# First norm of a 512-token model: shifts by GpSimd products summed on ScalarE, five early weight chunks accumulated feature by feature, the context loaded later

## The chip, the cores and the metric

The kernel runs on one core of a Trainium2 chip. TensorE multiplies matrices, VectorE and ScalarE work elementwise, GpSimd does so too, SyncE issues the loads. The metric is the device time of one execution in microseconds; the median of three runs counts.

## The reference

Two transformer blocks over 512 tokens of 1024 features. What matters here is the beginning: the first norm, modulated by a shift and a scale that come from the conditioning vector `c`, and the first feed-forward part, whose weights it meets.

```python
cond = jax.nn.silu(c)
mod = (cond @ ada_w[i] + ada_b[i]).reshape(B, N_SUB, N_MOD, D_MODEL)
shift, scale, gate = mod[:, :, 0], mod[:, :, 1], mod[:, :, 2]
h = modulate(rms_norm(x, norm_g[i, 0]), shift[:, 0], scale[:, 0])      # rms_norm(x) * (1 + scale) + shift
x = x + 0.5 * gate[:, 0, None, :] * swiglu(h, ffn_w_in[i, 0], ffn_w_out[i, 0])
...
a, b = jnp.split(h @ w_in, 2, axis=-1)                                 # swiglu
return (jax.nn.silu(a) * b) @ w_out
```

The second block also reads a context of 256 tokens (`ctx_2`), which it normalizes and modulates in the same way.

## The kernel before

The 1024 features lie on 8 tiles of 128 partitions (here: features 0 to 7), the 512 tokens along the free dimension. `x` is normalized by a row `nR` of reciprocal roots, which GpSimd makes by a power (`nr`) and TensorE spreads over the partitions. Each feature of the normed `h` is kept as two parts, `hh` rounded and `hl` the rest, and each weight chunk of 128x1024 likewise as `whi` (ScalarE) and `wlo` (VectorE); `mm3` makes three matmuls of 512 columns of each pair, and `proj` runs them over the 8 features into one output tile, so 24 matmuls for a chunk.

`first_norm` goes through the features k. It loads two slices of `ada_w` of 128x1024: `ads` for the scale, `adh` for the shift. The scale is a product with `cond` (the SiLU of `c`, on all partitions) that VectorE also sums up (`ada_col`). The shift of features 0 to 3 is made by TensorE instead: `adh` comes in another layout (`shift`) and 8 matmuls of one column multiply it with `ck`. That of features 4 to 7 goes by `ada_col`. Then VectorE adds the biases, makes the gain `gs`, and `norm_apply` gives `hn` (VectorE), `hh` (ScalarE) and `hl` (VectorE):

```python
nc.vector.scalar_tensor_tensor(u, src, gs[:, k:k + 1], R, ALU.mult, ALU.mult)
nc.scalar.activation(hi, u, AF.Identity, bias=sh[:, k:k + 1])
nc.vector.scalar_tensor_tensor(lo, u, sh[:, k:k + 1], hi.bitcast(F32), ALU.add, ALU.subtract)
```

Behind features 1 to 5 one chunk each of the first feed-forward weights is loaded and split (`PRELOAD_AT`); `ffn` takes these five as the chunks of its first three pairs j and loads the others itself. The pools hold 4 raw chunks and 5 split ones, and 6 output tiles. All loads are issued by SyncE in one order (`load`); `ctx_norm` issues the context's load with no such tie, and does the context's squares late in the second layer. The order in which the engines' instructions stand is set by a scheduler from the written order and their dependencies. In the rows, L204 to L206 are the three matmuls of `mm3`, L458 the matmuls of the shift, L249 and L250 `ada_col`, L462 the gain, L199 and L200 the split.

Of the kernel before, what the change touches and what calls it, by code (L numbers as in the profile page):

```python
# [9 lines left out]
F32 = mybir.dt.float32  # L10
F32R = mybir.dt.float32r
U8 = mybir.dt.uint8
AF = mybir.ActivationFunctionType
# [22 lines left out]
PRELOAD_AT = (1, 2, 3, 4, 5)  # L36
SHIFTS_ON_PE = 4
# [63 lines left out]
def layout(inp):  # L101
# [14 lines left out]
    out["shift"] = tiles(a["ada_w"][0, :, :D])  # L116
# [49 lines left out]
class Builder:  # L166
# [165 lines left out]
    def out_rows(self, load, xs, gate, slots=()):  # L332
        """tail(seg, acc): x += gate * (W^T xs) and its sums of squares, the last rows by segments."""
        ws, nt = [], min(TAIL, self.wbufs) + len(slots)

        def tail(seg, acc):
            if not ws:
                for m in range(KT - nt):
                    w = load(m)
                    ps = self.psum()  # L340
                    self.proj(ps, w, xs)
                    self.residual(m, ps, gate(), FULL, acc)
                own = list(slots) + [None] * (nt - len(slots))
                ws.extend(load(m, slots=own[m - KT + nt]) for m in range(KT - nt, KT))
            for m, w in zip(range(KT - nt, KT), ws):
                ps = self.psum()
                self.proj(ps[:, :seg[1]], w, xs, seg)
                self.residual(m, ps, gate(), seg, acc)

        return tail  # L350

# [1 line left out]
    def ffn(self, layer, s, h, gate, fill, mid=None):  # L353
        nc, d = self.nc, self.d
        tail = None
        for pi, (j0, n) in enumerate(PARTS):
# [12 lines left out]
            for grp in groups:  # L369
                w = {}  # L370
                for j in grp:
                    w[j] = [self.pre.pop(0) if self.pre else self.chunk(d["ffn_in"][layer, s, j0 + j, i]) for i in range(2)]
                    if j > 4:
                        self.order = None
                    gs.append(self.pair(j))
                for seg in (SEGS if len(grp) > 1 else (FULL,)):
                    for j in grp:
                        pa, pb = self.psum(), self.psum()
                        self.proj(pa[:, :seg[1]], w[j][0], h, seg)
                        self.proj(pb[:, :seg[1]], w[j][1], h, seg)  # L380
                        last = evac(pa, pb, gs[j], seg)
                for j in grp:
                    with self.tc.issue_after(last.ins):
                        fill()
# [37 lines left out]
    def load(self, dst, src):  # L422
        """A load on the sync queue; while self.order holds one, behind it."""
        if self.order is None:
            return self.nc.sync.dma_start(dst, src)
        with self.tc.issue_after(self.order):
            i = self.nc.sync.dma_start(dst, src)
        if not self.fixed:
            self.order = i.ins
        return i  # L430
# [5 lines left out]

    def first_norm(self):
        nc = self.nc
# [6 lines left out]
        ck = self.pmod.tile([P, 8], F32, name="ck")  # L445
        nc.scalar.activation(ck, self.vec("c"), AF.Silu)
        sc, sh = self.mod_tile(0, 1), self.mod_tile(0, 0)
        pre = list(PRELOAD_AT)
        ps = self.psum()
        for k in range(KT):  # L450
            i = k % 4
            self.ada_col(0, 1, k, self.pg.tile([P, D], F32, name=f"ads{i}", tag=f"g{2 * i}"))
            c = slice(k, k + 1)
            if k < SHIFTS_ON_PE:
                w = self.pg.tile([P, D], F32, name=f"adh{i}", tag=f"g{2 * i + 1}")
                self.load(w, self.d["shift"][k])
                for kk in range(KT):
                    nc.tensor.matmul(ps[:, c], w[:, kk * P:(kk + 1) * P], ck[:, kk:kk + 1], start=(kk == 0), stop=(kk == KT - 1))  # L458
                nc.vector.tensor_tensor(sh[:, c], ps[:, c], self.vec("ada_b", k, 1), ALU.add)
            else:  # L460
                self.ada_col(0, 0, k, self.pg.tile([P, D], F32, name=f"adh{i}", tag=f"g{2 * i + 1}"))
            nc.vector.scalar_tensor_tensor(gs[:, c], sc[:, c], 1.0, self.vec("norm_g", k, 1), ALU.add, ALU.mult)  # L462
            self.norm_apply(k, self.x[k], R, gs, sh, h[k][0], h[k][1])
            while pre and pre[0] == k:
                pre.pop(0)
                j, i = divmod(len(self.pre), 2)
                self.pre.append(self.chunk(self.d["ffn_in"][0, 0, j, i]))
# [145 lines left out]
    def ctx_norm(self):  # L613
# [4 lines left out]
        nc.sync.dma_start(ct, self.d["ctxT"])  # L618
# [91 lines left out]
    def first_values(self, H):  # L710
        """The first head's values and, in the same products, the low-rank gate inputs of all heads."""
# [464 lines left out]
    def setup(self):  # L1176
        nc, ctx, d = self.nc, self.ctx, self.d
        self.mod = {}
        self.pre = []
# [50 lines left out]
```

## Time and profile before

| | |
|---|---|
| median of 3 runs | 2787.91 us |
| lowest, highest | 2782.96, 2790.6 us |
| span of the profiled execution | 2789.4 us |
| TensorE busy in it | 2749.3 us (99%) |
| VectorE, ScalarE, GpSimd busy | 1534.0, 973.7, 30.7 us |
| HBM read | 344.42 MB |

The profiled execution's own time is its span, from its first to its last instruction. A busy TensorE is not TensorE at its peak; what it does in a stretch, and at which pace, is to be read beside it.

### The profile page before, as it was taken

Reading aid. Unit: us, or ns where it says so; the run is one execution under the profiler, and the core shown is the slowest. Engines: PE = TensorE matmul, PEld = TensorE weight load, DVE = VectorE, ACT = ScalarE, POOL = GpSimd, SP = SyncE. Lnnn points to the kernel's source line nnn. Section 1 sums busy time; section 2 is a strip of 40 time slices with the busy share of each in tenths; the row PEclk is TensorE's granted clock in tenths of the full one; section 3 lists DMA queues with packets and bytes.
Section 4 is the critical chain, followed back from the end, with each engine's and each line's share of the span. In section 5 each row is a group of like instructions: output and inputs, shape, how many; then the busy total and the mean of one; then the engine's idle time right before and its main releaser. Section 6 shows DMA issues by size and latency. Waiting matters only on the chain.

```text
span 2789.4 us, 35584 instructions
## 1 busy us (share of the span) xinstructions
PE 2749.3 (99%) x14437; PEld 2374.9 (85%) x14437; DVE 1534.0 (55%) x2553; ACT 973.7 (35%) x1509; POOL 30.7 (1%) x39
## 2 busy tenths in 40 slices
PE   7999999999999999999999999999999999999999
PEld 6888889888898888988988889999898888888887
DVE  6645577444575446744865545455456665454443
ACT  4222244222242222322432234444456652333222
POOL 0000000000000000000000000000000000000000
PEclk9999999999999999999999999999999999999999
DMA  8745543444545455332455433111121134323332
GB/s 313 249 147 184 190 128 129 144 145 132 161 134 184 153 164 171 107 100 91 154 185 163 154 103 121 54 35 39 46 80 53 57 109 145 97 92 93 103 95 81
DMA packets 102980, 354.60 MB, mean 127 GB/s; under 512 B 11424, under 2 KB 11680, under 8 KB 102688
## 3 DMA queue, kind: packets, MB, share of 16 engines
q1 hardware_dynamic: 100800, 348.66, 39.5%
q10 hardware_dynamic: 2016, 3.67, 0.3%
q8 instruction: 113, 1.85, 0.3%
q14 instruction: 51, 0.42, 0.0%
HBM read 344.42 MB, written 7.86 MB: 126 GB/s over the span
## 4 chain that ended last, share of the span: by engine, by line
PE 96%; ACT 1%; DVE 1%; DMA 1%; issue 0%; POOL 0%; SPq 0%; DVEq 0%; ACTq 0%
PE mm L204 28%; PE mm L206 28%; PE mm L205 28%; PE mm L871 1%; PE mm L872 1%; PE mm L873 1%; PE mm L966 1%; PE mm L1078 1%; PE mm L879 1%; PE mm L941 1%; PE mm L940 1%; ACT whi L199 0%; PE mm L458 0%; PE mm L504 0%; PE nR L285 0%
## 5 line engine op out<-in xcount | busy, mean ns | idle before, releaser
L204 PE MATMUL mm<-hh,wlo 128*128 128x512 f32 (+1 forms) x2344 | 881.1, 378 | 2.8 <-ACT hh L301 1.8
L205 PE MATMUL mm<-hh,whi 128*128 128x512 f32 (+1 forms) x2344 | 878.9, 377 | 0.0
L206 PE MATMUL mm<-hl,whi 128*128 128x512 f32 (+1 forms) x2344 | 870.0, 377 | 0.4 <-DVE hl L302 0.3
L199 ACT CAST whi<-wraw 128x1024 fp32r<-128x1024 f32 (+1 forms) x443 | 457.0, 1034 | 904.8 <-PE mm L206 484.9
L200 DVE TENSOR_TENSOR wlo<-wraw,whi 128x1024 fp32r<-128x1024 f32 (+1 forms) x443 | 533.0, 1205 | 314.4 <-ACT whi L199 312.0
L204 PEld LDWEIGHTS mm<-hh,wlo 128*128 128x128 f32 x2344 | 442.8, 189 | 81.2 <-ACT hh L301 2.2
L205 PEld LDWEIGHTS mm<-hh,whi 128*128 128x128 f32 x2344 | 442.4, 189 | 77.6
L206 PEld LDWEIGHTS mm<-hl,whi 128*128 128x128 f32 x2344 | 437.5, 189 | 80.2 <-DVE hl L302 0.8
L205 PE MATMUL mm<-g,whi 128*128 128x512 f32 (+1 forms) x1147 | 416.2, 363 | 0.0
L204 PE MATMUL mm<-g,wlo 128*128 128x512 f32 (+1 forms) x1147 | 416.0, 363 | 0.0
L206 PE MATMUL mm<-g,whi 128*128 128x512 f32 (+1 forms) x1147 | 413.7, 362 | 0.0
L205 PEld LDWEIGHTS mm<-g,whi 128*128 128x128 f32 x1147 | 216.5, 189 | 33.5
L206 PEld LDWEIGHTS mm<-g,whi 128*128 128x128 f32 x1147 | 216.5, 189 | 33.5
L204 PEld LDWEIGHTS mm<-g,wlo 128*128 128x128 f32 x1147 | 216.5, 189 | 33.4
L249 DVE SCALAR_TENSOR_TENSOR adaw<-adaw,cond 128x1024 f32<-128x1024 f32 x176 | 208.7, 1220 | 2.5 <-DMA adaw<-in_ada_dram 2.5
L324 DVE SCALAR_TENSOR_TENSOR x<-mm,hg,x 128x512 f32<-128x512 f32 (+1 forms) x115 | 76.2, 662 | 186.2 <-PE mm L206 186.2
L363 DVE TENSOR_TENSOR gf<-sa,mm 128x512 f32<-128x512 f32 (+1 forms) x94 | 61.3, 653 | 200.4 <-PE mm L206 191.8
L362 ACT ACTIVATE sa<-mm 128x512 f32<-128x512 f32 (+1 forms) x94 | 53.6, 570 | 316.2 <-PE mm L206 316.2
L324 DVE SCALAR_TENSOR_TENSOR x<-mm,mod,x 128x512 f32<-128x512 f32 (+1 forms) x56 | 37.8, 674 | 134.1 <-PE mm L206 134.1
L301 ACT ACTIVATE hh<-hn,mod 128x256 fp32r<-128x256 f32 (+1 forms) x120 | 58.4, 519 | 58.5 <-DVE hn L300 49.5
L269 DVE TENSOR_TENSOR nacc<-nacc,sq 128x256 f32<-128x256 f32 (+1 forms) x108 | 52.2, 486 | 27.7 <-ACT sq L268 27.2
L268 ACT ACTIVATE sq<-x 128x256 f32<-128x256 f32 (+1 forms) x90 | 42.1, 468 | 67.7 <-DVE x L324 64.2
(283 smaller groups left out, 2812.7 us busy)
## 6 DMA issues: line engine op xcount, KB each, us to landing
wraw<-in_ffn_in_dram SPq DMA_DIRECT2D x176, 512.0 KB, 3.6
adaw<-in_ada_dram SPq DMA_DIRECT2D x176, 512.0 KB, 4.6
wraw<-in_wm_dram SPq DMA_DIRECT2D x66, 512.0 KB, 3.6
wraw<-in_mlp_dram SPq DMA_DIRECT2D x64, 512.0 KB, 3.9
wraw<-in_ffn_out_dram SPq DMA_DIRECT2D x64, 448.0 KB, 3.4
wraw<-in_ffn_out_dram SPq DMA_DIRECT2D x32, 512.0 KB, 3.6
wraw<-in_conv_in_dram SPq DMA_DIRECT2D x24, 512.0 KB, 3.5
ads<-in_ada_dram SPq DMA_DIRECT2D x8, 512.0 KB, 10.0
```

Of the source, the lines that this page charges most:

```text
L199: self.nc.scalar.copy(hi, src)
L200: return self.nc.vector.tensor_tensor(lo, src, hi.bitcast(F32), ALU.subtract)
L204: mm(ps, wlo, xhi, start=start, stop=False)
L205: mm(ps, whi, xhi, start=False, stop=False)
L206: mm(ps, whi, xlo, start=False, stop=stop)
L249: nc.vector.scalar_tensor_tensor(out, raw, 1.0, self.cond[:, cond], ALU.mult, ALU.mult, accum_out=dst)
L268: nc.scalar.activation(sq[:, :n], src, AF.Square, scale=g)
L269: nc.vector.tensor_tensor(acc, acc, sq[:, :n], ALU.add)
L301: nc.scalar.activation(hi, u, AF.Identity, bias=sh[:, k:k + 1])
L324: self.nc.vector.scalar_tensor_tensor(x, ps[:, :seg[1]], gate[:, k:k + 1], x, ALU.mult, ALU.add)
L362: nc.scalar.activation(sa, pa[:, :seg[1]], AF.Silu)
L363: nc.vector.tensor_tensor(gf, sa, pb[:, :seg[1]], ALU.mult)
```

## The change

All eight shifts are made in one way, by `shift_col`: `adh` is loaded in the layout of `ads`, GpSimd multiplies it with `cond`, ScalarE copies the product in place and sums it along the way, VectorE adds the bias. The `shift` layout and `ck` go. Three chunks are loaded behind feature 0 and two behind feature 1 (`PRELOADS`). Each of these five chunks has an output tile of its own from then on, and after each feature `products` adds that feature's three matmuls to all five tiles; `ffn` finds the finished tiles in `early` (four are the first two pairs, the fifth is the first half of the third). The context's load is issued behind the last load that was written before it. Some comments go too, so lines have other numbers.

```diff
-PRELOAD_AT = (1, 2, 3, 4, 5)
-SHIFTS_ON_PE = 4
+PRELOADS = {0: 3, 1: 2}
...
-    out["shift"] = tiles(a["ada_w"][0, :, :D])
...
                 for j in grp:
-                    w[j] = [self.pre.pop(0) if self.pre else self.chunk(d["ffn_in"][layer, s, j0 + j, i]) for i in range(2)]
+                    early = [self.early.pop(0) if self.early else None for i in range(2)]
+                    w[j] = [None if early[i] else self.chunk(d["ffn_in"][layer, s, j0 + j, i]) for i in range(2)]
...
-                        pa, pb = self.psum(), self.psum()
-                        self.proj(pa[:, :seg[1]], w[j][0], h, seg)
-                        self.proj(pb[:, :seg[1]], w[j][1], h, seg)
+                        pa, pb = [early[i] or self.psum() for i in range(2)]
+                        for p, ww in zip((pa, pb), w[j]):
+                            if ww:
+                                self.proj(p[:, :seg[1]], ww, h, seg)
...
+    def shift_col(self, m, raw):
+        nc = self.nc
+        self.load(raw, self.d["ada"][0][m])
+        dst = self.mod_tile(0, 0)[:, m:m + 1]
+        nc.gpsimd.tensor_tensor(raw, raw, self.cond[:, 0], ALU.mult)
+        nc.scalar.activation(raw, raw, AF.Copy, accum_out=dst)
+        nc.vector.tensor_tensor(dst, dst, self.vec("ada_b", m, 1), ALU.add)
...
-        ck = self.pmod.tile([P, 8], F32, name="ck")
-        nc.scalar.activation(ck, self.vec("c"), AF.Silu)
         sc, sh = self.mod_tile(0, 1), self.mod_tile(0, 0)
-        pre = list(PRELOAD_AT)
-        ps = self.psum()
+        rows, done = [], []
+        def products(upto):
+            for i, w in enumerate(rows):
+                while done[i][1] < upto:
+                    k = done[i][1]
+                    s = slice(k * P, (k + 1) * P)
+                    self.mm3(done[i][0], w[0][:, s], w[1][:, s], h[k][0], h[k][1], k == 0, k == KT - 1)
+                    done[i][1] += 1
         for k in range(KT):
...
-            if k < SHIFTS_ON_PE:
-                w = self.pg.tile([P, D], F32, name=f"adh{i}", tag=f"g{2 * i + 1}")
-                self.load(w, self.d["shift"][k])
-                for kk in range(KT):
-                    nc.tensor.matmul(ps[:, c], w[:, kk * P:(kk + 1) * P], ck[:, kk:kk + 1], start=(kk == 0), stop=(kk == KT - 1))
-                nc.vector.tensor_tensor(sh[:, c], ps[:, c], self.vec("ada_b", k, 1), ALU.add)
-            else:
-                self.ada_col(0, 0, k, self.pg.tile([P, D], F32, name=f"adh{i}", tag=f"g{2 * i + 1}"))
+            self.shift_col(k, self.pg.tile([P, D], F32, name=f"adh{i}", tag=f"g{2 * i + 1}"))
...
-            while pre and pre[0] == k:
-                pre.pop(0)
-                j, i = divmod(len(self.pre), 2)
-                self.pre.append(self.chunk(self.d["ffn_in"][0, 0, j, i]))
+            for _ in range(PRELOADS.get(k, 0)):
+                j, i = divmod(len(rows), 2)
+                rows.append(self.chunk(self.d["ffn_in"][0, 0, j, i]))
+                done.append([self.psum(), 0])
+            products(k + 1)
+        self.early = [ps for ps, _ in done]
         return h
...
         ct = self.pg.tile([P, KT, C], F32, name="ctxt")
-        nc.sync.dma_start(ct, self.d["ctxT"])
+        with self.tc.issue_after(self.last_load.ins):
+            nc.sync.dma_start(ct, self.d["ctxT"])
```

On VectorE, where the last features are made (ads2 and adh2 belong to feature 6, ads3 and adh3 to feature 7, hn_315 and hl5 to feature 5), before:

```order
L249 SCALAR_TENSOR_TENSOR ads2_325,mod0_1_186<-ads2_325,cond_127 128x1024
L250 TENSOR_TENSOR mod0_0_187<-mod0_0_187,vecs_79 128x1
L462 SCALAR_TENSOR_TENSOR gs00_183<-mod0_1_186,vecs_79 128x1
L249 SCALAR_TENSOR_TENSOR adh2_329,mod0_0_187<-adh2_329,cond_127 128x1024
L250 TENSOR_TENSOR mod0_1_186<-mod0_1_186,vecs_79 128x1
L300 SCALAR_TENSOR_TENSOR hn_315<-x5_85,gs00_183,nR_162 128x512
L249 SCALAR_TENSOR_TENSOR ads3_338,mod0_1_186<-ads3_338,cond_127 128x1024
L250 TENSOR_TENSOR mod0_0_187<-mod0_0_187,vecs_79 128x1
L462 SCALAR_TENSOR_TENSOR gs00_183<-mod0_1_186,vecs_79 128x1
L249 SCALAR_TENSOR_TENSOR adh3_342,mod0_0_187<-adh3_342,cond_127 128x1024
L302 SCALAR_TENSOR_TENSOR hl5_180<-hn_315,mod0_0_187,hh5_172 128x512
```

and with the change (ads2 is feature 6, ads3 feature 7):

```order
L473 SCALAR_TENSOR_TENSOR gs00_183<-mod0_1_184,vecs_79 128x1
L298 SCALAR_TENSOR_TENSOR hn_376<-x5_85,gs00_183,nR_162 128x512
L247 SCALAR_TENSOR_TENSOR ads2_395,mod0_1_184<-ads2_395,cond_127 128x1024
L300 SCALAR_TENSOR_TENSOR hl4_179<-hn_347,mod0_0_185,hh4_171 128x512
L248 TENSOR_TENSOR mod0_1_184<-mod0_1_184,vecs_79 128x1
L445 TENSOR_TENSOR mod0_0_185<-mod0_0_185,vecs_79 128x1
L473 SCALAR_TENSOR_TENSOR gs00_183<-mod0_1_184,vecs_79 128x1
L298 SCALAR_TENSOR_TENSOR hn_405<-x6_86,gs00_183,nR_162 128x512
L247 SCALAR_TENSOR_TENSOR ads3_424,mod0_1_184<-ads3_424,cond_127 128x1024
L300 SCALAR_TENSOR_TENSOR hl5_180<-hn_376,mod0_0_185,hh5_172 128x512
L248 TENSOR_TENSOR mod0_1_184<-mod0_1_184,vecs_79 128x1
```

The products of `adh` are gone from here, the bias of the shift stays (mod0_0), and hl of a feature stands behind hn of the next and ads of the one after it.

On GpSimd, the eight products stand between the power of the first norm and that of the second.

On ScalarE, at the end of the first norm (hh6 and hh7 are the last features, cond the SiLU of the two other conditioning vectors, mm_356 the tile of the first chunk, whi the sixth chunk and its followers), before:

```order
L435 ACTIVATE cond_127<-cond_127 128x1024 x2
L301 ACTIVATE hh6_173<-hn_334,mod0_0_187 128x512
L301 ACTIVATE hh7_174<-hn_347,mod0_0_187 128x512
L362 ACTIVATE sa_406<-mm_356 128x512
L199 CAST whi_492<-wraw_490 128x1024
L199 CAST whi_567<-wraw_565 128x1024
L199 CAST g0_355<-gf_407 128x512
L362 ACTIVATE sa_476<-mm_426 128x512
```

and with the change (the ACTIVATE on adh sums a shift, mm_206 is the first early chunk's tile, whi_494 the sixth chunk):

```order
L444 ACTIVATE adh2_399,mod0_0_185<-adh2_399 128x1024
L299 ACTIVATE hh6_173<-hn_405,mod0_0_185 128x512
L436 ACTIVATE cond_127<-cond_127 128x1024
L444 ACTIVATE adh3_428,mod0_0_185<-adh3_428 128x1024
L436 ACTIVATE cond_127<-cond_127 128x1024
L299 ACTIVATE hh7_174<-hn_434,mod0_0_185 128x512
L360 ACTIVATE sa_458<-mm_206 128x512
L197 CAST whi_494<-wraw_492 128x1024
L360 ACTIVATE sa_478<-mm_220 128x512
L197 CAST whi_544<-wraw_542 128x1024
```

The sums of the shifts have come in between, and the cast of the sixth chunk stands behind the SiLU of the first tile in both.

On TensorE, at the same place, with the change (mm_206, 213, 220, 250 and 257 are the five early tiles, mm_499 that of the sixth chunk):

```order
L203 MATMUL mm_220<-hh7_174,whi_216 128x512
L202 MATMUL mm_250<-hh7_174,wlo_247 128x512
L203 MATMUL mm_250<-hh7_174,whi_246 128x512
L202 MATMUL mm_257<-hh7_174,wlo_254 128x512
L203 MATMUL mm_257<-hh7_174,whi_253 128x512
L204 MATMUL mm_206<-hl7_182,whi_202 128x512
L204 MATMUL mm_213<-hl7_182,whi_209 128x512
L204 MATMUL mm_220<-hl7_182,whi_216 128x512
L204 MATMUL mm_250<-hl7_182,whi_246 128x512
L204 MATMUL mm_257<-hl7_182,whi_253 128x512
L202 MATMUL mm_499<-hh0_167,wlo_495 128x512
L203 MATMUL mm_499<-hh0_167,whi_494 128x512
```

Before, a chunk ran over several features in a row, and a chunk was done when it had met all eight:

```order
L204 MATMUL mm_426<-hh0_167,wlo_284 128x512
L205 MATMUL mm_426<-hh0_167,whi_283 128x512
L206 MATMUL mm_426<-hl0_175,whi_283 128x512
L204 MATMUL mm_426<-hh1_168,wlo_284 128x512
L205 MATMUL mm_426<-hh1_168,whi_283 128x512
L206 MATMUL mm_426<-hl1_176,whi_283 128x512
L204 MATMUL mm_426<-hh2_169,wlo_284 128x512
L205 MATMUL mm_426<-hh2_169,whi_283 128x512
```

So all five tiles now end within five matmuls of each other, and the sixth chunk begins right behind them.

## Rows read from the trace of the kernel before

**Rows 1.** Busy us (x instructions) by stretch, then granted clock, DMA share, GB/s.
```profile
0.00:14.30 14.30, 1.87 (x8) 1.78 (x8) 5.01 (x10) 8.76 (x12) 0.34 (x6) 1.00 0.87 305
14.30:43.10 28.80, 26.38 (x98) 23.88 (x99) 23.43 (x48) 8.53 (x10) 1.94 (x1) 1.00 1.02 391
43.10:53.20 10.10, 10.10 (x46) 8.34 (x45) 9.87 (x23) 4.08 (x5) 0.00 (x0) 1.00 0.98 395
53.20:65.00 11.80, 11.80 (x54) 9.77 (x53) 4.89 (x7) 5.43 (x8) 0.00 (x0) 1.00 0.16 47
```

**Rows 2.** Chain that ended last, around 43 us: start us, us, what.
```profile
42.85 0.43 PE mm L204
...
47.63 0.45 PE mm L206 x2
```

**Rows 3.** TensorE's groups to 65 us: xcount | busy us, mean ns.
```profile
L206 PE MATMUL mm<-hl,whi 128*128 128x512 f32 x40 | 15.8, 437 | 0.0
L458 PE MATMUL mm<-ck,adh 128*128 128x1 f32 x64 | 13.8, 346 | 0.2 <-DVE mod L459 0.2
```

**Rows 4.** Timeline of ScalarE at 65 us: start us, us, instruction, [idle before <-releaser].
```profile
64.96 0.60 ACT L362 ACTIVATE sa<-mm 128x512 f32<-128x512 f32 x1 [0.34 <-PE mm L206]
```

**Rows 5.** VectorE's groups in the first 62 us.
```profile
L249 DVE SCALAR_TENSOR_TENSOR ads<-ads,cond 128x1024 f32<-128x1024 f32 x8 | 9.8, 1220 | 0.1
L200 DVE TENSOR_TENSOR wlo<-wraw,whi 128x1024 fp32r<-128x1024 f32 x7 | 8.5, 1222 | 0.1
L300 DVE SCALAR_TENSOR_TENSOR hn<-x,gs,nR 128x512 f32<-128x512 f32 x8 | 6.0, 744 | 1.4 <-PE nR L285 1.3
L302 DVE SCALAR_TENSOR_TENSOR hl<-hn,mod,hh 128x512 fp32r<-128x512 f32 x8 | 5.9, 747 | 0.1
...
L250 DVE TENSOR_TENSOR mod<-mod,vecs 128x1 f32<-128x1 f32 x12 | 1.9, 155 | 0.1
L462 DVE SCALAR_TENSOR_TENSOR gs<-mod,vecs 128x1 f32<-128x1 f32 x8 | 1.2, 155 | 0.1
```

**Rows 6.** ScalarE's groups in the first 62 us.
```profile
L199 ACT CAST whi<-wraw 128x1024 fp32r<-128x1024 f32 x7 | 7.2, 1041 | 6.3 <-DMA wraw<-in_ffn_in_dram 6.3
L301 ACT ACTIVATE hh<-hn,mod 128x512 fp32r<-128x512 f32 x8 | 5.8, 724 | 19.6 <-DVE hn L300 10.8 <-DVE mod L459 8.9
```

**Rows 7.** ScalarE's groups in the whole span, by shape.
```profile
L1067 ACT ACTIVATION_READ_ACCUMULATOR probs<-sc,mx,rs 128x1 f32 x32 | 6.8, 211 | 0.0
```

**Rows 8.** GpSimd's groups in the whole span, by shape.
```profile
L280 POOL TENSOR_TENSOR nr<-nm,mhalf 128x2 f32<-128x2 f32 x13 | 9.2, 710 | 1617.6 <-DVE nm L279 1528.2 <-DVE mod L250 89.4
L280 POOL TENSOR_TENSOR qr<-qm,mhalf 128x4 f32<-128x4 f32 x8 | 8.4, 1055 | 139.0 <-DVE mx L1069 110.2 <-DVE qm L279 15.1 <-DVE mx L1066 13.7
...
L667 POOL MEMSET lrT<- 128x768 f32 x1 | 0.7, 738 | 0.0
```

**Rows 9.** Timeline of VectorE and GpSimd where a power runs, at three places.
```profile
14.32 1.23 DVE L249 SCALAR_TENSOR_TENSOR ads<-ads,cond 128x1024 f32<-128x1024 f32 x1
14.48 1.94 POOL L280 TENSOR_TENSOR nr<-nm,mhalf 128x4 f32<-128x4 f32 x1 [13.61 <-DVE nm L279]
...
797.62 0.88 DVE L302 SCALAR_TENSOR_TENSOR hl<-hn,mod,hh 128x256 fp32r<-128x256 f32 x2
797.63 0.70 POOL L280 TENSOR_TENSOR nr<-nm,mhalf 128x2 f32<-128x2 f32 x1 [10.70 <-DVE nm L279]
...
2097.71 0.68 DVE L1098 TENSOR_TENSOR sw<-sw,rope 128x512 f32<-128x512 f32 x1
2097.88 1.39 POOL L280 TENSOR_TENSOR qr<-qm,mhalf 128x4 f32<-128x4 f32 x1 [14.61 <-DVE qm L279]
```

**Rows 10.** Timeline before the context's norm.
```profile
1418.92 1.47 SPq L425 DMA_DIRECT2D adaw<-in_ada_dram  x2
...
1426.64 0.61 ACT L199 CAST g<-gf 128x512 fp32r<-128x512 f32 x1
```

**Rows 11.** DMA issues by line: count, KB each, median us to landing.
```profile
adaw<-in_ada_dram SPq DMA_DIRECT2D x176, 512.0 KB, 4.6
```

More of the change, by code (lines that the diff above doesn't have):

```diff
@@ L424, in load @@
         if self.order is None:
-            return self.nc.sync.dma_start(dst, src)
+            self.last_load = self.nc.sync.dma_start(dst, src)
+            return self.last_load
         with self.tc.issue_after(self.order):
-            i = self.nc.sync.dma_start(dst, src)
+            i = self.last_load = self.nc.sync.dma_start(dst, src)
         if not self.fixed:
@@ L1178, in setup @@
         self.mod = {}
-        self.pre = []
+        self.early = []
         self.order, self.fixed = None, False
```

## Prediction

> **What bounds the kernel now.** I read the windows first, then the chain that ended last, then the groups by line. TensorE is busy nearly without a break from 18 us to the end; what the change touches is the first 65 us. In the stretch 14.3 to 43.1 us the reader is to see three things at once [rows 1]: TensorE 26.4 of 28.8 us busy, VectorE 23.4 of 28.8, and the loads at 391 GB/s with a DMA share of 1.02. GpSimd is nearly idle there (1.9 us). From 43.1 to 53.2 VectorE is full (9.9 of 10.1). From 53.2 on only TensorE is full: VectorE has handed over the last feature and TensorE works off what has piled up.
>
> TensorE's busy time hides two losses. A matmul of 512 columns takes 0.43 us until 43.1 us and 0.23 after it [rows 2], the paces of 1.2 and 2.4 GHz. And of its time up to 65 us, 13.8 us go to the 64 one-column matmuls of the four shifts [rows 3]. The chain runs over both.
>
> The two kernels are best compared at one point: when five weight chunks have met all eight features, which is 5 x 8 x 3 = 120 matmuls. Before, that is at 64.9: line 206 has 40 starts by 65 us [rows 3], and the SiLU of the third pair's first output, the fifth chunk, starts at 64.96 right after a matmul of line 206 [rows 4]. Behind this point both programs have nearly the same order, and TensorE is the only bound. So the change is worth 65.0 minus the time at which the changed kernel starts its 121st matmul.
>
> **What is removed.** The 64 one-column matmuls go, 13.8 us of TensorE. On VectorE, four shift sums by product and accumulation (features 4 to 7, 1.22 us each, the same form as the scale rows of [rows 5]) go: 4.9 us. The context's 1 MB leaves the early queue; at 391 GB/s [rows 1] that is 2.7 us of transfer. None of this is a gain by itself, since in the new order TensorE waits for each feature anyway.
>
> **What is added, feature by feature.** A GpSimd product of 128x1024, a ScalarE sum, a bias on VectorE. ScalarE's sum costs like the other 128x1024 passes, 1.04 us [rows 6], and 0.21 for reading the accumulator [rows 7]: 1.25.
>
> The product has no row in this trace. The nearest rows are those of GpSimd [rows 8]. A memset of 768 columns takes 0.74 us, so 1024 columns of one stream take 0.98: the lower end. The powers take 0.71 us for 2 columns and 1.06 for 4, which leaves 0.37 us that does not depend on the columns. Two operands that come in one behind the other take 0.37 + 2 x 0.98 = 2.3; with the result as a third stream in turn 3.3, the upper end. (A power's 0.17 us a column would make 175 us; that is its own iteration, and the memset's row excludes that this engine needs it for plain columns.) I take 2.3, two streams in and the result beside them.
>
> The Trainium skill, in "GPSIMD Engine Reference", section "Elementwise — side-by-side cycle accounting", speaks against this change: a two-input tensor_tensor runs there at about half VectorE's speed, 4497 ns for 2048 columns. By that the product would be an estimated 2.25 us and the sum below would come out 0.4 us lower. No run here shows it yet.
>
> **The interface that GpSimd and VectorE share.** The first power starts at 14.48 while VectorE multiplies ads by cond, two tensors from SBUF, until 15.55, and takes 1.94 us; another of the same form at 2097.88 beside sw by rope takes 1.39 [rows 9]; the usual one takes 1.06 [rows 8]. The excess of 0.9 and 0.3 is about what was left of the VectorE row. One pair does not show it: at 797.63, 0.01 us behind a VectorE row, the power takes its usual 0.70 [rows 9]. So GpSimd waits for a VectorE operation with two SBUF operands. Whether VectorE waits in turn for a GpSimd product of 2 us, no row shows, since the powers read 2 to 4 columns. I assume that it does, symmetrically. The Trainium skill says so too ("SBUF — State Buffer", section "Who interferes with whom": whoever starts first holds the shared pair for the whole instruction); the power at 14.48 agrees for one direction.
>
> **The sum.** On the shared interface stand, per feature: the product (2.3), ads (1.22), hl (0.75), the scale's bias and gain (0.16 each) and the shift's bias (0.16) [rows 5]; hn reads one operand from PSUM and fits beside the product. That is 4.75 us, less about 0.1 for the overlap of VectorE's own rows, 4.6 per feature. The five low parts of the chunks (1.22 each) come on top, all before the fifth product.
> - The first power ends at 16.4 [rows 9], the first product at 18.7, its sum at 20.0, hh of feature 0 at 21.6: TensorE's first real matmul comes at 21.7. On the interface, from 16.4 to the fifth product: four products 9.2, three ads 3.7, five low parts 6.1, two hl 1.5, small rows 1.3, and 0.6 in which neither has its input: 22.4, so 38.8.
> - Three features more at 4.6: the eighth product runs from 52.7 to 55.0.
> - Behind it VectorE has the last ads (1.22), an hl (0.75) and small rows until 57.3. On ScalarE stand then, in order, hh of feature 6 (0.72), the SiLU of one extra cond row (1.04), the last sum (1.25), the second SiLU (1.04) and hh of feature 7 (0.72) [rows 6, 7]; with the bias on VectorE and hand-overs of 0.05 to 0.1 us, hh of feature 7 is ready at 61.8.
> - TensorE has kept up: 15 matmuls a feature at 0.227 are 3.4 us against 4.6, and it takes the last 15 until 65.3.
> - Then a new wait. All five weight slots are held until the last feature, so the sixth chunk can be rounded only when the first chunk's last product is done, eleven matmuls into the last feature (64.4). ScalarE stands behind a SiLU (0.60 [rows 4]), then the cast (1.04), then VectorE's low part (1.22), and four hand-overs of about 0.05: the 121st matmul starts at 67.4, 2.1 us after the 120th has ended. Later chunks take two to three us on ScalarE and VectorE against 5.5 of TensorE, so the wait does not come back.
>
> Against 65.0 the change loses 2.4 us. The profiled execution's span is 2789.4, 1.5 above the median of 2787.9; I forecast on the median: 2787.9 + 2.4 = **2790.3 us**.
>
> The loads don't bind: up to the eighth adh they are 13.8 MB, of which 305 GB/s brings 4.4 by 14.3 us and 391 GB/s the rest in 24 us [rows 1]; it could land near 39 and is wanted at 52.7. The early chunks' casts on ScalarE hide between the sums. If VectorE were not the slower, these would show.
>
> **The context later.** Its load is now issued just behind the load at 1418.92 [rows 10]. A load of half a megabyte takes 4.6 us to land [rows 11]; twice the size, 1.3 us more: 1425 to 1426. ScalarE has three context squares queued ahead of the last cast of g, which before ran at 1426.64 [rows 10]. It would run near 1429. TensorE begins the next output about a microsecond before the cast's old place, at 1425.7, and needs this g for its last of eight steps, 21 matmuls or 4.8 us on: at 1430.5. Cost nothing; if the load came 2 us later than that, what it is late by, so 0 to 2 us.
>
> **Rivals.**
> - *No hold-up between VectorE and GpSimd.* For it: the one power at 797.63. Then features come every 3.4 us, the last hh at 49.0, and TensorE, still at the low pace until the middle thirties, is the bound: 27 matmuls at 0.43, 93 at 0.227 and 2 us of waits from 21.7 end near 56.4, and the 121st starts at 58.5. That is 6.5 us faster, 2781.4. Should the clock rise as late as before (43.1), some 3 us less.
> - *The product is longer, the kernel slower.* Each 0.1 us of the product comes eight times, 0.8 us. At 3.3, with three streams in turn, it loses 2.4 + 8 = 10.4: 2798. It is slower by over 0.3% from 3.05 us on. Against it: the memset's pace would allow even one stream.
> - *TensorE stays at the low pace.* Before, the pace rose after matmuls of 512 columns without a break from 37.5 to 43.1; now there are waits between features. At 0.43 a feature takes 6.4 us, longer than the 4.6 between features, so the waits vanish and the engine is as busy as it was then; that speaks against it. If it stayed, 120 matmuls from 21.7 would end at 74 and the loss be 11: 2799.
>
> **How the numbers follow.** Forecast (hold-up in both directions, product 2.0 to 2.6 us, 2787 to 2793): 0.60. No hold-up: 0.22. Longer product: 0.12. Low pace or a late context: 0.06. A change of 0.3% is 8.4 us, about what a measurement of this kernel can tell from no change. The no-hold-up case passes that only with luck (a quarter of it, with a short wait for the sixth chunk), so faster is 0.07; slower takes the long product for the most part and the low pace, 0.15; the rest, 0.78, is within 0.3%. The range holds the forecast and the no-hold-up case and reaches into the longer product: 2780 to 2798. The forecast's own range is 2787 to 2794.
>
> **What would show it.** The products: eight GpSimd rows of 2.0 to 2.6 us (below 2.0 or above 3.0 and the term is wrong). The hold-up: VectorE rows of ads and hl in the first 60 us that are longer than 1.22 and 0.75, or start late, where a product runs; and products longer than the shortest where VectorE works. Without both, the first rival. The last hh at about 61.8, four to five us between features. A TensorE gap of about 2 us between hl of feature 7 and the sixth chunk's low part, released by VectorE. A context load that lands by 1426 and no TensorE gap there. The prediction is wrong where the 121st matmul starts before 57 or after 73.

## Result and profile after

| | before | after |
|---|---|---|
| median of 4 runs each | 2788.2 us | 2833.55 us (2829.4 to 2834.5) |
| ratio, 95% interval | | 1.0162 [1.0146, 1.0179] |
| span of the profiled execution | 2789.4 us | 2832.1 us |
| 121st product starts | 64.7 us | 70.8 us |
| span behind it | 2724.7 us | 2761.3 us |

The changed kernel is 1.6% slower; forecast was 2790.3 us, with a range to 2798. The table splits the 42.7 us between the two profiles at the prediction's own point of comparison: 6.1 us are lost ahead of the 121st product, and 36.6 us behind it, where the prediction had both kernels at one pace.

**The first 70 us.** In the changed kernel L202 to L204 are the three matmuls of `mm3`, L443 to L445 the product, the sum and the bias of a shift. Windows, in the columns of [rows 1]:

```profile
14.30:43.10 28.80, 15.20 (x38) 9.27 (x38) 25.67 (x23) 9.58 (x13) 21.64 (x8) 1.00 0.76 299
43.10:53.20 10.10, 8.10 (x24) 6.45 (x25) 10.03 (x23) 5.29 (x9) 2.41 (x1) 0.66 0.71 249
53.20:65.00 11.80, 11.80 (x53) 9.46 (x52) 6.17 (x17) 6.04 (x9) 0.00 (x0) 1.00 0.68 277
```

Against [rows 1] TensorE's busy time from 14.3 to 43.1 us falls from 26.4 to 15.2 us, and GpSimd's rises from 1.9 to 21.6. The granted clock of the next stretch is 0.66, where it was 1.00. Next the groups on GpSimd and VectorE up to 62 us (GpSimd's to 65), with count, busy us and mean ns; [rows 5] has the same forms before:

```profile
L443 POOL TENSOR_TENSOR adh<-adh,cond 128x1024 f32<-128x1024 f32 x8 | 22.3, 2805 | 13.9 <-DMA adh<-in_ada_dram 13.9
```
```profile
L247 DVE SCALAR_TENSOR_TENSOR ads<-ads,cond 128x1024 f32<-128x1024 f32 x8 | 11.2, 1396 | 0.0
L300 DVE SCALAR_TENSOR_TENSOR hl<-hn,mod,hh 128x512 fp32r<-128x512 f32 x8 | 10.2, 1275 | 1.4 <-ACT hh L299 1.4
L198 DVE TENSOR_TENSOR wlo<-wraw,whi 128x1024 fp32r<-128x1024 f32 x5 | 9.7, 1947 | 0.3 <-ACT whi L197 0.3
L298 DVE SCALAR_TENSOR_TENSOR hn<-x,gs,nR 128x512 f32<-128x512 f32 x8 | 6.0, 747 | 2.8 <-PE nR L283 2.6
```

hl goes from 747 to 1275 ns in the mean and wlo from 1222 to 1947; hn, which has one operand in PSUM, is at 747 (744 before). The means mix held and free ones, so the timeline of VectorE and of GpSimd shows single ones (start us, us):

```profile
21.66 2.85 DVE L300 SCALAR_TENSOR_TENSOR hl<-hn,mod,hh 128x512 fp32r<-128x512 f32 x1
...
27.76 2.70 DVE L198 TENSOR_TENSOR wlo<-wraw,whi 128x1024 fp32r<-128x1024 f32 x1
30.39 2.31 DVE L445 TENSOR_TENSOR mod<-mod,vecs 128x1 f32<-128x1 f32 x1
```
```profile
21.31 2.66 POOL L443 TENSOR_TENSOR adh<-adh,cond 128x1024 f32<-128x1024 f32 x1 [2.94 <-DMA adh<-in_ada_dram]
27.02 2.36 POOL L443 TENSOR_TENSOR adh<-adh,cond 128x1024 f32<-128x1024 f32 x1 [3.06 <-DMA adh<-in_ada_dram]
29.59 6.47 POOL L443 TENSOR_TENSOR adh<-adh,cond 128x1024 f32<-128x1024 f32 x2 [0.21 <-DMA adh<-in_ada_dram]
```

hl, begun 0.35 us behind a product that ends at 23.97, takes 2.85 us and ends 0.54 behind it; a bias of one column takes 2.31 us in place of 0.16. The products in turn are 2.34 us at the least, and 3.1 to 3.4 in three that start while such a VectorE row runs. So the hold-up goes both ways. The Trainium skill has it that the two contend ("SBUF — State Buffer", section "Who interferes with whom": a VectorE instruction with two SBUF inputs and a GpSimd instruction that reads SBUF contend). This trace agrees with it.

The features come unevenly by this. From 29.6 to 42.1 us GpSimd runs four products in a row, and VectorE gets through five rows with two SBUF operands. hh is ready at 21.1, 33.4, 45.0, 47.7, 50.6, 54.9, 57.7 and 61.3 us: that of feature 2 is 24 us behind that of feature 0, and the other five come within 16. The eighth product then waits for its load, which is issued right behind ScalarE's sum of feature 3 (begun at 44.96 us), since it overwrites the tile that this sum reads:

```profile
44.33 0.72 ACT L299 ACTIVATE hh<-hn,mod 128x512 fp32r<-128x512 f32 x1 [9.84 <-DVE mod L445]
...
44.96 1.04 ACT L444 ACTIVATE adh<-adh 128x1024 f32<-128x1024 f32 x1
...
45.10 0.80 PE L202 MATMUL mm<-hh,wlo 128*128 128x512 f32 x1 [3.70 <-ACT hh L299]
...
46.12 0.33 SPq L428 DMA_DIRECT2D adh<-in_ada_dram  x1
...
49.81 2.41 POOL L443 TENSOR_TENSOR adh<-adh,cond 128x1024 f32<-128x1024 f32 x1 [7.66 <-DMA adh<-in_ada_dram]
```

From hh of feature 2 at 45.1 us to the end of the 120th product TensorE has no idle time; this window holds the last 90 of the 120:

```profile
45.10:68.84 23.74, 23.74 (x90) 18.66 (x90) 14.47 (x32) 11.45 (x19) 2.41 (x1) 0.88 0.61 239
```

The end of this stretch, on TensorE, with the wait for the sixth chunk:

```profile
67.51 1.33 PE L204 MATMUL mm<-hl,whi 128*128 128x512 f32 x5
70.78 0.58 PE L202 MATMUL mm<-hh,wlo 128*128 128x512 f32 x1 [1.94 <-DVE wlo L198]
```

And windows of the granted clock around the products (its column is the third from the end):

```profile
36.93:43.76 6.83, 3.11 (x11) 1.72 (x10) 6.83 (x8) 0.00 (x0) 5.21 (x2) 1.00 0.17 71
43.76:50.58 6.82, 5.48 (x13) 4.32 (x14) 6.75 (x18) 4.26 (x8) 0.77 (x1) 0.50 0.68 217
50.58:71.06 20.48, 18.54 (x80) 14.62 (x79) 11.04 (x21) 10.19 (x16) 1.64 (x1) 1.00 0.52 210
71.06:74.48 3.42, 3.42 (x9) 2.65 (x9) 3.42 (x6) 3.42 (x6) 0.00 (x0) 0.50 0.60 168
```

From 43.76 to 50.58 us 0.50 was granted, the level of 1.2 GHz; TensorE was idle from 41.4 to 45.1. It fell again at 71.06, behind the idle 1.94 us. In the first of these falls TensorE is busy for 5.48 us; half of that, 2.7 us, is lost ahead of the 121st product: without it that would have started at 68.0.

**Behind it.** The order is nearly the one before, and TensorE shows no new waits of any size. What differs is the pace. The windows of before, then of after, in one stretch where the moving operand is hh or hl and one where it is g:

```profile
178.00:255.00 77.00, 77.00 (x341) 63.75 (x340) 49.07 (x87) 21.57 (x28) 0.00 (x0) 1.00 0.65 211
257.00:290.00 33.00, 33.00 (x147) 27.32 (x146) 12.22 (x13) 7.77 (x8) 0.00 (x0) 1.00 0.38 112
```
```profile
178.00:255.00 77.00, 77.00 (x331) 61.85 (x330) 44.57 (x77) 20.53 (x27) 0.00 (x0) 1.00 0.60 192
257.00:290.00 33.00, 33.00 (x147) 27.30 (x146) 16.04 (x21) 7.15 (x9) 0.00 (x0) 1.00 0.44 144
```

In both kernels TensorE is busy all the time at a granted clock of 1.00. Before, it gets through 341 products in 77 us, after through 331; with g as the moving operand it is 147 in 33 us in both. "100% busy" hides this. What shows it is the number of products in a fixed stretch, and with it the busy time of the weight loads (63.75 and 61.85 us), or the distance between two starts. From all neighbouring rows of the traces, the mean from start to start of 512-column products on hh and hl is 227.0 ns before and 233.33 after, and of those on g 226.7 and 226.9.

**Where the tiles lie.** In the built kernels hh0 starts at byte 18336 of its SBUF partition both before and after. Between the h pool and the weights lies the mod pool, and the change takes the 32-byte tile ck out of it. All that is allocated behind it moves down by 32 bytes: a whi tile from byte 114592 to 114560, and g, the raw chunks and the rest likewise. All hh and hl tiles are 2048 bytes long and the weight slices 512, so the distance between a moving operand and a weight slice was 0 before, counted in 256 bytes, and is 32 after. Between g and the weights, which moved together, it is 0 in both.

### The profile page after: what moved, and what is told of

It is laid out like the page before. It is cut to its first block, busy times and chain, and to the rows that moved or that the text cites. A ratio compares the mean times of both kernels' runs of the same rounds, so it can differ in the third digit from the quotient of the medians.

```text
span 2832.1 us, 35464 instructions
## 1 busy us (share of the span) xinstructions
PE 2777.4 (98%) x14373; PEld 2357.3 (83%) x14373; DVE 1542.7 (54%) x2545; ACT 981.0 (35%) x1524; POOL 52.9 (2%) x47
## 4 chain that ended last, share of the span: by engine, by line
PE 95%; DVE 2%; ACT 2%; DMA 1%; issue 1%; POOL 0%; SPq 0%; DVEq 0%; ACTq 0%
PE mm L202 28%; PE mm L203 28%; PE mm L204 28%; PE mm L885 1%; PE mm L887 1%; PE mm L886 1%; PE mm L980 1%; PE mm L893 1%; PE mm L1092 1%; DVE wlo L198 1%; PE mm L955 1%; PE mm L954 1%; ACT whi L197 1%; PE mm L517 0%; PE sc L1076 0%
## 5 line engine op out<-in xcount | busy, mean ns | idle before, releaser
L202 PE MATMUL mm<-hh,wlo 128*128 128x512 f32 (+1 forms) x2344 | 893.5, 383 | 15.9 <-ACT hh L299 9.9
L203 PE MATMUL mm<-hh,whi 128*128 128x512 f32 (+1 forms) x2344 | 891.2, 382 | 0.0
L204 PE MATMUL mm<-hl,whi 128*128 128x512 f32 (+1 forms) x2344 | 877.8, 382 | 3.1 <-DVE hl L300 3.0
L202 PEld LDWEIGHTS mm<-hh,wlo 128*128 128x128 f32 x2344 | 441.9, 189 | 111.5 <-ACT hh L299 11.8
L204 PEld LDWEIGHTS mm<-hl,whi 128*128 128x128 f32 x2344 | 436.0, 188 | 97.1 <-DVE hl L300 4.7
L202 PE MATMUL mm<-g,wlo 128*128 128x512 f32 (+1 forms) x1147 | 416.1, 363 | 0.0
L204 PE MATMUL mm<-g,whi 128*128 128x512 f32 (+1 forms) x1147 | 414.0, 363 | 0.0
L204 PEld LDWEIGHTS mm<-g,whi 128*128 128x128 f32 x1147 | 216.5, 189 | 33.7
L202 PEld LDWEIGHTS mm<-g,wlo 128*128 128x128 f32 x1147 | 216.5, 189 | 33.6
L361 DVE TENSOR_TENSOR gf<-sa,mm 128x512 f32<-128x512 f32 (+1 forms) x94 | 61.3, 653 | 216.8 <-PE mm L204 202.5
L267 DVE TENSOR_TENSOR nacc<-nacc,sq 128x256 f32<-128x256 f32 (+1 forms) x108 | 52.1, 485 | 27.3 <-ACT sq L266 26.8
L300 DVE SCALAR_TENSOR_TENSOR hl<-hn,mod,hh 128x256 fp32r<-128x256 f32 (+1 forms) x120 | 61.1, 534 | 9.7 <-ACT hh L299 9.3
```

Source lines behind the costliest of these rows:

```text
L202: mm(ps, wlo, xhi, start=start, stop=False)
L203: mm(ps, whi, xhi, start=False, stop=False)
L204: mm(ps, whi, xlo, start=False, stop=stop)
L267: nc.vector.tensor_tensor(acc, acc, sq[:, :n], ALU.add)
L361: nc.vector.tensor_tensor(gf, sa, pb[:, :seg[1]], ALU.mult)
```

## The experiments

Three theories for the 36 us behind the 121st product. **Placement**: a 512-column product is slower when its moving operand and the weights lie at different offsets. **Order**: the pace comes from the new order of the first 70 us, other PSUM banks or other code. **Clock**: falls of the granted clock. The clock is small from the outset. Halving the time at 0.50 between the 121st product and the last gives 5.1 us lost before and 6.8 after, so 1.7 of the 36.6. "Rest" below is the span behind the 121st product less this loss: 2719.6 us before, 2754.5 after. Every kernel in this part computes the whole reference. The intervals are of the ratio to the kernel before.

**e1, the changed kernel with the 32 bytes put back.**
```diff
         gs = self.pmod.tile([P, 8], F32, name="gs00")
+        pad = self.pmod.tile([P, 8], F32, name="pad")
```


> The changed kernel with one unused tile of 32 bytes a partition put where the tile ck was, so that everything behind the mod pool lies where it lay before; instructions and their order are those of the changed kernel. Placement theory (a 512-column matmul is slower when the rows of its moving operand and the weight tiles lie an odd multiple of 32 bytes apart in SBUF): start to start of the products on hh and hl goes back from 233.33 to 226.67 ns, the drift behind 120 us (about 34 us) is gone, time about 2799 us (2795 to 2804), what is left above before being the 9 to 10 us of the first 120 us. Rival (the pace comes from the new order of the first 70 us, the other PSUM banks or the other code): 233.33 ns stays, 2833 us.

Measured: 2795.32 us, ratio 1.0027 [1.0017, 1.0036]; rest 2718.7. One unused tile of 32 bytes takes back 38 of the 45 us. The pace is that of before, 341 products in the window:

```profile
178.00:255.00 77.00, 77.00 (x341) 63.75 (x341) 48.10 (x85) 19.99 (x27) 0.00 (x0) 1.00 0.65 206
```

**e2, the kernel before without the 32 bytes.**
```diff
-        ck = self.pmod.tile([P, 8], F32, name="ck")
-        nc.scalar.activation(ck, self.vec("c"), AF.Silu)
+        ck = self.vec("c")
+        nc.scalar.activation(ck, ck, AF.Silu)
```


> The kernel before, with ck written over the columns of vecs that it is computed from and no tile of its own, so that everything behind the mod pool lies 32 bytes lower; nothing else differs. Placement theory: the first 65 us are as before, then 233.33 ns in all products on hh and hl, time about 2788 + 34 to 38 = 2822 to 2826 us. Rival (order, banks or code): 2788 us.

Measured: 2825.92 us, 1.0137 [1.0121, 1.0153]. The 121st product starts at 64.8 as before, and the rest is 2754.3: the loss without any of the change. Its window:

```profile
178.00:255.00 77.00, 77.00 (x333) 61.96 (x332) 47.06 (x84) 19.65 (x26) 0.00 (x0) 1.00 0.62 202
```

The theory of order falls with e1 and e2 together.

**e3, the weights 64 bytes lower.** As e2, and gs00 is written over the scales (`gs = sc`).

> The kernel before, 64 bytes lower behind the mod pool: ck over vecs, and gs00 written over the scales that it is computed from. Placement theory with a period of 64 bytes: 226.67 ns, 2788 us as before. With a period of 128 bytes or more, or if any shift of the weights costs: 233.33 ns or another pace, 2822 us or so. Rival (order, banks or code): 2788 us.

Measured: 2797.13 us, 1.0037 [1.0021, 1.0053], rest 2729.2; 229.2 ns on hh and hl. Neither of the two times named: in the rest a shift of 64 bytes costs 9.6 us, 28% of what 32 cost.

**e4, hh and hl 32 bytes higher, the weights in place.**
```diff
-        ck = self.pmod.tile([P, 8], F32, name="ck")
+        ck = self.cp.tile([P, 8], F32, name="ck")
```


> The kernel before, with the tile ck taken from the const pool in place of the mod pool: now hh and hl lie 32 bytes higher and the weights where they were, so the two are again an odd multiple of 32 bytes apart, but the other way round (hh on a multiple of 64, weights not). Placement theory by distance: 233.33 ns on hh and hl, 2822 to 2826 us. Placement theory by the moving operand's or the weights' own address alone (hh off a multiple of 64 with weights on one is slow): 226.67 ns, 2788 us. Rival (order, banks or code): 2788 us.

Measured: 2823.32 us, 1.0122 [1.0101, 1.0143], rest 2754.4; 233.33 ns. The weights' own address cannot be it, since they didn't move; nor can a start off a multiple of 64, since hh and hl now lie on one and are slower. It is the distance between the two, in either direction.

**e9 and e10, hh and hl 128 and 256 bytes higher.** As e4, with gs00 and two (six) of layer 0's modulation vectors moved into the const pool too.

> The kernel before, with four tiles of 32 bytes (ck, gs00 and the first norm's shifts and scales) taken from the const pool in place of the mod pool: hh and hl lie 128 bytes higher, the weights where they were. In the placed and displaced kernels so far a distance of 0 gave 226.7 ns, 32 bytes either way 233.33, 64 bytes 229.2. If the pace depends on the distance with a period of 128 bytes: 226.7 ns on hh and hl, 2788 us. If the period is 256 bytes or more (the merge stage of the kernel before has moving tiles that lie 128 bytes off, at 231 to 232 ns): 229 to 232 ns, 2800 to 2815 us.

Measured: 2824.44 us, 1.0138 [1.0124, 1.0152], rest 2753.4; 233.0 ns, slower than the 229 to 232 that the merge stage suggested.

> As the last, with eight tiles of 32 bytes moved (the first norm's and four more modulation vectors of layer 0): hh and hl 256 bytes higher. Period of 256 bytes: 226.7 ns and 2788 us. Period of 512 bytes or more: 229 to 234 ns, 2800 to 2826 us.

Measured: 2788.35 us, 1.0002 [0.9992, 1.0013], rest 2719.0; 227.0 ns. So 256 bytes count as none. The windows of e3, e4, e9 and e10:

```profile
178.00:255.00 77.00, 77.00 (x339) 63.20 (x338) 48.36 (x86) 20.62 (x28) 0.00 (x0) 1.00 0.66 211
```
```profile
178.00:255.00 77.00, 77.00 (x333) 62.08 (x332) 48.49 (x86) 20.79 (x28) 0.00 (x0) 1.00 0.63 205
```
```profile
178.00:255.00 77.00, 77.00 (x333) 62.20 (x332) 48.47 (x86) 20.88 (x28) 0.00 (x0) 1.00 0.65 205
```
```profile
178.00:255.00 77.00, 77.00 (x342) 63.75 (x341) 49.46 (x87) 21.59 (x28) 0.00 (x0) 1.00 0.65 211
```

| distance of moving operand and weights, bytes | kernels | start to start, ns | rest, us |
|---|---|---|---|
| 0 | before, e1 | 227.0 | 2719.6, 2718.7 |
| 32, either way | after, e2, e4 | 233.33 | 2754.5, 2754.3, 2754.4 |
| 64 | e3 | 229.2 | 2729.2 |
| 128 | e9 | 233.0 | 2753.4 |
| 256 | e10 | 227.0 | 2719.0 |

The products of 256 columns on hh (608 of them) rank otherwise: in the mean 121.1 ns from start to start at 0 (before), 118.2 at 32 (e2), 118.8 at 64, 120.1 at 128 and 121.1 at 256.

The next five ask what the change itself is worth with the tiles at distance 0.

**e5, the changed kernel, padded, its shifts on VectorE.**
```diff
-            self.shift_col(k, self.pg.tile([P, D], F32, name=f"adh{i}", tag=f"g{2 * i + 1}"))
+            self.ada_col(0, 0, k, self.pg.tile([P, D], F32, name=f"adh{i}", tag=f"g{2 * i + 1}"))
```


> The changed kernel with its 32 bytes put back, and all eight shift products as one VectorE instruction each (the ada_col of the kernel before) in place of GpSimd's product and ScalarE's sum. If GpSimd's product with the hold-up of VectorE beside it sets the pace of the features: VectorE's sum is 8 x 4.6 + 5 x 1.22 = 43 us behind 14 us, the last hh at 56 in place of 60 us, the 121st product at 63 in place of 67 us, time 3 to 5 us below the padded kernel, 2790 to 2792 us. If VectorE's own work is as long as the hold-up was (rival): 121st at 67 us or later, 2795 us.

Measured: 2786.06 us, 0.9993 [0.9984, 1.0002]. The last hh is ready at 51.3 us and the 121st product starts at 60.0 (in e1 60.8 and 67.3), some 3 to 5 us earlier than expected; the time is 9 us below e1's. The wait for the sixth chunk has shrunk to 0.16 us:

```profile
59.96 0.50 PE L202 MATMUL mm<-hh,wlo 128*128 128x512 f32 x1 [0.16 <-DVE wlo L198]
```

GpSimd's product costs VectorE more than it takes off it: as VectorE's own work the eight products take 1.22 us each, and hl and wlo are back at 751 and 1220 ns.

**e6, the early chunks alone.** The changed kernel with the shifts of the kernel before: ck, four features on TensorE, four on VectorE.

> The changed kernel with the shifts of the kernel before (four on TensorE, four on VectorE, ck in its place): the early chunks accumulated feature by feature and the later context alone. If the five output tiles are worth what TensorE's idle time of the first 43 us suggests: VectorE's sum is 4 x 3.3 + 4 x 4.6 + 5 x 1.22 = 38 us behind 14 us, the last hh at 51 us, the 121st product at 57 to 60 in place of 65 us, time 2780 to 2783 us. Rival (the loads set the end: rows of feature 7 land at 49 us or later, and the wait for the sixth chunk stays): 121st at 62 to 65 us, 2785 to 2788 us.

Measured: 2789.84 us, 1.0005 [0.9996, 1.0015]; last hh at 52.1, 121st product at 60.9. TensorE gets there 3.8 us earlier than in the profile of before, as the gain would have it, but the time shows none.

**e7, the shifts alone.** The kernel before with shift_col for all eight shifts, its five early chunks as they were.

> The kernel before with all eight shifts by GpSimd products summed on ScalarE, the six early chunks multiplied one after the other as before, the tile ck left in place unused. If the products set the last hh at 60 to 62 us whatever the chunks do: behind it TensorE still has some four chunks of 24 products (22 us) to do, the 121st at 80 to 84 us, time 2803 to 2807 us. Rival (the hold-up needs the accumulation's order to matter, so that the shifts alone cost as little as the whole change in the placed kernel): 2790 to 2796 us.

Measured: 2795.32 us, 1.0022 [1.0013, 1.0032]; last hh at 63.2, 121st product at 69.6. My 80 to 84 was wrong: I had the early chunks one behind the other, which would leave four of them undone when the last hh comes. But 98 products have ended by 65 us: they run as features come, in the kernel before's code too. So accumulating by feature was less new than the code looked.

**e8, all eight shifts on TensorE.** As e6, with `SHIFTS_ON_PE = 8`.

> The changed kernel with all eight shifts as TensorE products with ck (the first four are so in the kernel before), nothing on GpSimd, ck in its place. VectorE's sum is 8 x 3.3 + 5 x 1.22 = 33 us behind 14 us; if it sets the pace, the last hh at 47 to 50 us, TensorE's 120 products at 52 to 54, the 121st at 55 to 58 us with the wait for the sixth chunk, time 2778 to 2781 us, below both kernels. Rival (the loads or TensorE's own order, whose shift products wait for loads ahead of products that are ready, set the end): 121st at 62 us or later, 2785 to 2788 us.

Measured: 2800.51 us, 1.0049 [1.0033, 1.0064]; last hh at 67.0, 121st product at 72.7. The rival held:

```profile
L481 PE MATMUL mm<-ck,adh 128*128 128x1 f32 x128 | 18.2, 269 | 0.5 <-DVE mod L482 0.5
```

The 64 one-column matmuls, 128 rows in the trace, take 18.2 us of TensorE, and stand in one queue with the products of the chunks, while hh waits for them: the last six of feature 7's shift start at 65.3 us, its hh is ready at 67.0.

**e11, the context later, alone.** The kernel before with the changed load of ctxT.

> The kernel before with only the context's load issued behind the last load that stands ahead of it. If it is hidden, as the prediction has it: 2788 us, no new idle time of TensorE over 0.8 us between 1150 and 1450 us. Rival (the later landing holds ScalarE's squares and what stands behind them): an idle time of TensorE there of 1 to 7 us, 2789 to 2795 us.

Measured: 2786.3 us, 1.0 [0.9991, 1.0009]; no such idle time of TensorE. The load is issued at 1418.2 and takes 7.3 us, so it lands at 1425.5.

**e12, two shifts on TensorE, six on VectorE.** As e6, with `SHIFTS_ON_PE = 2`.

> The run with all shifts on VectorE, but the first two features' shifts on TensorE, where it is idle anyway (idle 1.3 to 2.7 us at 13 to 33 us there). If VectorE's first features are what TensorE waits for: hh of features 1 to 3 come 1 to 2.4 us earlier, the 121st product at 58 to 59.5 in place of 60.0 us, 2784 to 2785 us, below the kernel before by 0.1%. Rival (TensorE's 16 shift products, which waited for their loads, cost it as much): 60 to 61 us, 2786 to 2788 us.

Measured: 2784.89 us, 0.9992 [0.9983, 1.0001]; 121st product at 60.5. In the profile nothing is gained over e5. It is the lowest median of all, and still not measurably below before.

**e13 and e14, what is left in e1.** The padded kernel measures 8.5 us above before, where its profile has only 2.6 at the 121st product. e13 is that kernel again; e14 adds 22 products into an output tile that nobody reads, behind features 0 to 3, so that TensorE idles less.

> The padded changed kernel a second time, for its profile. Its first profile had no fall of the granted clock in the first 100 us and started the 121st product at 67.3 us; the changed kernel's profile had falls to 0.50 at 43.8 and 71.1 us and started it at 70.8. If these falls are chance and are what the medians hold above the forecast (2795.3 against 2790.3): falls of 3.4 to 6.8 us somewhere from 40 to 110 us in this profile, with the 121st product later by half of what falls before it. If the cause is anything else: no fall there, the 121st at 67.3 again, and a time near 2795 us nevertheless.

Measured: 2796.49 us, 1.003 [1.0021, 1.004]. This time the profile has falls to 0.50 at 46.0, 69.8 and 411.2 us, the 121st product at 69.25, and a span of 2798.8 where the first had 2791.1. The falls come and go between executions of one kernel:

```profile
46.00:49.40 3.40, 3.40 (x9) 2.64 (x8) 3.36 (x10) 1.76 (x3) 0.00 (x0) 0.51 0.64 202
69.80:73.20 3.40, 3.40 (x10) 2.60 (x9) 3.40 (x5) 3.40 (x6) 0.00 (x0) 0.51 0.62 187
```

> The padded changed kernel with 22 extra matmuls of 512 columns into an output tile that nobody reads (4, 8, 6 and 4 behind the products of features 0 to 3), so that TensorE waits less there. Theory of the clock (the waits of the first 45 us let the granted clock fall in most executions): no fall in the first 100 us, the 121st product at 66.5 to 67.5 us, time 2790 to 2792 us, 3 to 5 us below the padded kernel of the same call. Rival (no such falls in most executions, or the extra matmuls delay the real ones): as the padded kernel or slower, 2795 us or more.

Measured: 2796.87 us, 1.0031 [1.0022, 1.0041], as the padded kernel. The clock fell all the same, to 0.50 from 33.4 to 40.2 us, and the 121st real product started at 69.3. So the fillers don't hold the clock, and the theory that they would has failed.

## Why the prediction was wrong

**The step that failed** is "Behind this point both programs have nearly the same order, and TensorE is the only bound. So the change is worth 65.0 minus the time at which the changed kernel starts its 121st matmul." The order is nearly the same, and TensorE is the only bound; but the same products need not have the same pace. The change drops ck, which has nothing to do with them, and 32 bytes of SBUF with it. That costs 34.9 us of the 42.7 between the profiles (rest 2754.5 against 2719.6); e2 shows the same loss without the change, and e1 takes it back. The 6,000 products of 512 columns on hh and hl behind the 121st at 6.3 ns more make 37.8 us; the 912 of 256 columns, at 2.8 ns less, take 2.6 off. Where the pace is equal, the step holds: over the ten other profiles at distance 0 or 256 (e1, e5 to e8, e10 to e14) the rest is 2718.7 to 2720.7 us, beside before's 2719.6, whatever the 121st product's start (60.0 to 72.7).

**The sum up to the 121st product** had its terms nearly right, and its end too, but the way to that end was another, so that the end fits is in part luck.
- One-column matmuls: the 64 that I counted for four shifts are rows; the program has 32, with two rows each. Their 13.8 us are right.
- Product: forecast 2.3 us, measured 2.34 undisturbed, 2.81 in the mean. The figure of the Trainium skill ("GPSIMD Engine Reference", section "Elementwise — side-by-side cycle accounting"), halved, made it an estimated 2.25; the trace agrees within 0.1 us.
- The symmetric hold-up: assumed, and shown; the rival without it is out. The longer product is out as well.
- Pace of the features: forecast four to five us apart; measured 12.3 and 11.6 us, then 2.7 to 4.3.
- "The loads don't bind": GpSimd waits 13.9 us for loads, 7.7 of them ahead of the eighth product. It runs from 49.8 to 52.2 us, where the forecast had 52.7 to 55.0.
- "TensorE has kept up": it has not. It works without a break from hh of feature 2 to the 120th product, for 23.7 us here and for 20.7 in e1 (44.6 to 65.3 us). So hh of feature 2 and TensorE's own pace set the end, and hh of feature 7 comes before TensorE has room for it. The forecast had e1's 65.3 too, but by hh of feature 7 and 15 products behind it: luck.
- hh of feature 7: forecast 61.8, measured 61.3, and 60.8 and 61.6 in the two padded profiles.
- Wait for the sixth chunk: forecast 2.1, measured 1.94.
- 121st product: forecast 67.4; 67.3 in e1, where the clock didn't fall; 69.25 in e13 and 70.8 in the changed kernel, where it did.
- Early chunks that cost nothing and a loss that is all of the shifts: e6 and e7 agree with it.
- The context: forecast to land at 1425 to 1426 and cost nothing; e11 has 1425.5 and no difference. The load took 7.3 us in place of 4.6 + 1.3 = 5.9, and was issued at 1418.2, ahead of the 1418.92 that I counted from, so the landing is right by two errors that cancel.

**The clock.** My rival had TensorE staying at the low pace, with the argument that slow products close the waits. It rose, at 37.5 us; what I left out is that it falls again behind a wait, for 3.4 or 6.8 us in these profiles. In the changed profile that costs 2.7 us ahead of the 121st product, and the slower pace of the 90 products there another 0.6.

**What stays open.** e1 and e13 together are 8.5 to 9 us above before in time, against the 2.4 forecast; the intervals leave 4.7 at the least. The falls account for the 7.7 us between the two padded profiles for the larger part: three more in the first 420 us at 1.7 us each. But the mean granted clock over all executions of both is 0.9975 against 0.9981 before, which is worth 1.7 us, and at the same mean clock of 0.998 nine padded executions have 2794.9 us in the mean and 19 of before beside them 2788.4. The remainder may lie in before's own point of comparison. In seven profiles of before's order (before, e2, e3, e4, e9 to e11) the 121st product starts at 63.9 to 64.8 in five and at 61.1 and 61.2 in two (e4 and e9), where TensorE's pace rose 8 us sooner (34 to 35 in place of 42 to 43 us). The 65.0 that I compared with is thus on the late side. That this is the rest is argued, not shown, since executions without a profile have no such row.

## What to carry to other kernels

A change that adds or drops even a 32-byte tile moves every buffer behind it; compare the addresses of both kernels before saying that the rest runs as before. Count the products in a fixed stretch, since a TensorE that is 100% busy at full granted clock may still be 3% slower. When a forecast time comes out, check the steps on the way as well: here the end fitted though the features and TensorE went another way. And a product moved to an idle GpSimd is not free if VectorE reads two SBUF operands beside it: here VectorE would sooner have done it itself.

## What the hardware showed that I had not expected

The pace of a 128x512 fp32r product depends on how far its moving operand lies from its weights in SBUF, within 256 bytes: 227.0 ns at 0 and 256, 233.33 at 32, 229.2 at 64, 233.0 at 128. At 256 columns 0 is no longer the best: 121.1 ns on hh against 118.2 at 32. The Trainium skill ("SBUF — State Buffer", section "Who interferes with whom") calls TensorE's two read ports, for the moving operand and for the weights, independent. A pace that changes with the offset between the two operands speaks against that, but what it is that the reads meet in no run here shows. In the merge stage of the kernel before, 125 products at distance 128 and 126 at distance 64 have 231.4 and 234.3 ns in the mean. That is not the 233.0 and 229.2 of hh and hl at these distances, so the distance alone does not fix the pace; why is open. Aligning them too would be worth an estimated 125 x 4.4 + 126 x 7.3 = 1.5 us. It wasn't tried.
